# Projections by feature as three 256-column products in one PSUM bank, in place of a 512-column and a 256-column product whose halves VectorE adds

## The chip, the cores and the metric

The kernel runs on one core of a Trainium2 chip. The metric is the device time of one execution in microseconds; the times given are medians of several executions, and the profile is of one execution.

## The reference

The reference is one decoder layer with two parallel token mixers on 256 tokens of width 2048. All of it is in float32.

```python
h = rms_norm(x, pre_norm_w)                       # (256, 2048)
proj = h @ w_in                                   # one projection, 12304 columns
gdn_qkv, gdn_z, gdn_b, gdn_a, moba_qkv, moba_z, gate_a, gate_b = split(proj)
# A: causal depthwise conv (4 taps) and SiLU on q, k, v; l2-normed q, k;
#    gated delta rule in chunks of 64 tokens, 8 heads of 128; gated RMS norm
qkv = silu(causal_depthwise_conv(gdn_qkv, conv_w))
u_a = gated_rms(gated_delta_rule(...), gdn_z) @ w_branch_a
# B: causal softmax attention, 8 heads of 128 (one block of 256 tokens)
u_b = (attention(qb, kb, vb) * silu(moba_z)) @ w_branch_b
merged = sigmoid(gate_a) * u_a + sigmoid(gate_b) * u_b
out = x + rms_norm(merged @ w_out, post_norm_w)
```

## The kernel before

Every large product is made with operands that are split in two: a value is rounded to `hi` (float32r), and `lo` is the rest. A product is then hi·hi + hi·lo + lo·hi. `split` (L220) does this for weights: ScalarE copies to `hi` (L225), VectorE subtracts to get `lo` (L226). The normed and transposed input is held the same way in `hT`: for each of the 16 k-tiles of 128 input features, 512 columns, of which the first 256 (`S`, one for each token) are the high part and the last 256 the low part.

There are two kinds of projection. `proj_n` (L358) is by token: the input is the stationary operand, the weights stream, and three products of up to 512 columns for each k-tile and each half of the tokens add up in one bank. `proj_t` (L340) is by feature: the weights are stationary (128 features) and the tokens stream, because the convolution along the tokens and the scores need features on partitions. It handles 256 columns of `w_in`, that is two heads (`m`), in two loads of eight k-tiles (`kb`). For each k-tile `hi` is multiplied with all 512 columns of `hT`, so that hi·hi lies in the left half of the bank and hi·lo in the right, and `lo` with the first 256 columns, added to the left half:

```python
mm(pts[m], hi[:, kk, :], hT[:, k, :], start=(k == 0), stop=False)
mm(pts[m][:, :S], lo[:, kk, :], hT[:, k, :S], start=False, stop=(k == KT - 1))
```

Afterwards `halves` (L459) adds the two halves of the bank: ScalarE copies the right one to SBUF (L461), VectorE adds the left one (L462). `conv_silu` (L465) then multiplies by the tokens' norm factor `rrow` into a padded row `xp` (L468), and makes the four taps and the SiLU in place. `keys` (k), `queries` (q) and `values` (v) do that for the first mixer. `attention` (L1077) takes the queries `mq` as they come from `halves`, and the keys `mk` scaled by `rrow` (L1084). `attend` makes the scores `ms` from them later. The first four heads' keys come from `first_products` (L282), which is written out at the start of the kernel: four 512-wide products for the four heads of a k-tile, then four 256-wide ones; they use `halves` too.

The order of the blocks is the list `ORDER` (L42), beginning with q0, mv0, zg0, q1 and so on; `proj_t` is called 18 times (q, v, mq and mk four times each, k twice). All TensorE instructions keep program order (`mm`, `tr`, L146 to L150). Smaller work (scores, the inverse, attention, weighting) stands in queues of generators (`Queue`, L47) that are advanced by `tick` every few products, so it is interleaved with the projections by count of products, not by time. The other engines' instructions are put in order by a scheduler, unless they are pinned. PSUM has four banks of 512 columns for the projections (`acc`) and four for the rest (`aux`). Weights are loaded by the sync engine's queue, one megabyte at a time, into three buffers.

Of the kernel before, what the change touches and what calls it, by code (L numbers as in the profile page):

```python
# [8 lines left out]
F32 = mybir.dt.float32  # L9
# [3 lines left out]
ALU = mybir.AluOpType  # L13
AX = mybir.AxisListType

P = 128
# [58 lines left out]
def hybrid_layer(  # L75
# [15 lines left out]
    nc = tc.nc  # L91
    B, S, D = x.shape
    NT = S // P
    KT = D // P
    H = a_log.shape[1]
    HD = gdn_norm_w.shape[1]
    GW = H * HD
    NTAP = conv_w.shape[1]
# [21 lines left out]
    wf = early.enter_context(tc.tile_pool(name="wf", bufs=8))  # L120
# [3 lines left out]
    def acc_tile(name):  # L124
        return acc.tile([P, 512], F32, tag="acc", name=name)
# [4 lines left out]
    gq, vq, mq = Queue(), Queue(), Queue()  # L130
# [8 lines left out]
    def tick():  # L139
        after[0] -= 0.5  # L140
        for q in (gq, vq, mq, *(() if held else aq + bq), *extra):
            q.tick()
# [3 lines left out]
    def mm(*args, **kwargs):  # L146
        return pin(nc.tensor.matmul(*args, **kwargs))  # L147
# [72 lines left out]
    def split(raw, shape, name):  # L220
        splits[0] += 1
        pool = fourth[0] if fourth and splits[0] % 4 == 0 else wspl
        hi = pool.tile(shape, F32R, tag="hi", name=f"hi_{name}")
        lo = pool.tile(shape, F32R, tag="lo", name=f"lo_{name}")
        nc.scalar.copy(hi, raw)  # L225
        nc.vector.tensor_tensor(lo, raw, hi.bitcast(F32), op=ALU.subtract)  # L226
        return hi, lo
# [5 lines left out]
    hT = big.tile([P, KT, 2 * S], F32R, tag="hT", name="hT")  # L233
# [3 lines left out]
    def turn(c):  # L237

        pts = []
        for k in range(4 * c, 4 * c + 4):  # L240
            if k % 2 == 0:
                pt = aux_tile(f"hTp_{k}")
            pts.append((k, pt[:, k % 2 * S : (k % 2 + 1) * S]))
            for t in range(NT):
                tr(pts[-1][1][:, t * P : (t + 1) * P], xs[t][:, k * P : (k + 1) * P], ident)
        return pts
# [48 lines left out]
    pts = turn(0)  # L295
# [26 lines left out]
    rrow = cst.tile([P, S], F32, name="rrow")  # L322
# [16 lines left out]

    def proj_t(col, name):  # L340

        pts = [acc_tile(f"a_{name}_{m}") for m in range(2)]
        for kb in range(2):
            raw = wraw.tile([P, 8, 256], F32, tag="raw", name=f"raw_{name}_{kb}")
            nc.sync.dma_start(
                raw, w_in[kb * 1024 : (kb + 1) * 1024, col : col + 256].rearrange("(k p) c -> p k c", p=P)
            )
            for m in range(2):
                hi, lo = split(raw[:, :, m * P : (m + 1) * P], [P, 8, P], f"{name}_{kb}_{m}")
                for kk in range(8):  # L350
                    k = kb * 8 + kk
                    mm(pts[m], hi[:, kk, :], hT[:, k, :], start=(k == 0), stop=False)
                    mm(pts[m][:, :S], lo[:, kk, :], hT[:, k, :S], start=False, stop=(k == KT - 1))
                    if kk % 4 == 3:
                        tick()
        return pts
# [27 lines left out]
    late = []  # L384
# [71 lines left out]
        decaying.pop()  # L456


    def halves(pt, name):  # L459
        y = wf.tile([P, S], F32, tag="f256", name=f"y_{name}")  # L460
        nc.scalar.copy(y, pt[:, S:])  # L461
        nc.vector.tensor_tensor(y, pt[:, :S], y, op=ALU.add)  # L462
        return y

    def conv_silu(y, m, late=None):  # L465
        xp = xps[xpi[0] % 3]
        xpi[0] += 1
        nc.vector.tensor_tensor(xp[:, NTAP - 1 :], y, rrow, op=ALU.mult)  # L468
        nc.scalar.activation(y, xp[:, 0:S], AF.Copy, scale=pcol[:, m : m + 1])
        for j in range(1, NTAP):  # L470
            nc.vector.scalar_tensor_tensor(
                y, xp[:, j : j + S], pcol[:, j * NCV + m : j * NCV + m + 1], y, op0=ALU.mult, op1=ALU.add
            )
        if late is None:
            nc.scalar.activation(y, y, AF.Silu)
        else:
            late.append(lambda: pin(nc.scalar.activation(y, y, AF.Silu)))
# [26 lines left out]
    def score_pair(h, kT, qT):  # L504
        kqs = []
        for m in range(2):
            kq = big.tile([P, 2, 2 * S], F32R, tag=("tt", "tw")[m], name=f"kq_{h + m}")
            for i, y in enumerate((kT[m], qT[m])):
                nc.scalar.copy(kq[:, i, :S], y)
                nc.vector.tensor_tensor(kq[:, i, S:], y, kq[:, i, :S].bitcast(F32), op=ALU.subtract)  # L510
            kqs.append(kq)
        yield SC_WAIT
        for m in range(2):
            yield from scores(h + m, kqs[m], qT[m])

        for b in range(4):
            t, p_ = b // 2, b % 2
            c0 = t * 4 * P + p_ * 64
            nc.gpsimd.dma_start(
                l_d[b, h : h + 2].rearrange("h j i -> j h i"),  # L520
                gsl[h // HG][p_ * 64 : p_ * 64 + 64, h % HG : h % HG + 2, c0 : c0 + 64],
            )
# [78 lines left out]
    kTs = [[] for _ in range(H // 2)]  # L601

    def keys(p):
        pk = proj_t(CK + 2 * p * P, f"k{2 * p}")
        kTs[p] += [halves(pk[m], f"k{2 * p + m}") for m in range(2)]
        for m in range(2):
            conv_silu(kTs[p][m], H + 2 * p + m)

    def queries(p):
        h = 2 * p  # L610
        pq = proj_t(CQ + h * P, f"q{h}")
        qTs = [halves(pq[m], f"q{h + m}") for m in range(2)]
        for m in range(2):
            conv_silu(qTs[m], h + m)
        gq.add(score_pair(h, kTs[p], qTs))
        if p == H // 2 - 1:
            gq.add(inverse())
            gq.add(solve())
# [60 lines left out]
    def v_tok(h, vT):  # L679
        yield V_WAIT if h % 2 == 0 else 0.5  # L680
        while sc_left[0]:
            yield 1
        pv = aux_tile(f"vt_{h}")
        for t in range(NT):
            tr(pv[:, t * P : (t + 1) * P], vT[:, t * P : (t + 1) * P], ident)
        nc.vector.tensor_tensor(
            gvt[h // HG][:, :, h % HG, :],
            pv[:, : 2 * P].rearrange("p (t e) -> p t e", t=NT),
            sk[:, :, h : h + 1].to_broadcast([P, NT, P]),
            op=ALU.mult,  # L690
        )
# [3 lines left out]
    def values(p):  # L695
        h = 2 * p
        pv_ = proj_t(CV + h * P, f"v{h}")
        vTs = [halves(pv_[m], f"v{h + m}") for m in range(2)]
        for m in range(2):
            conv_silu(vTs[m], 2 * H + h + m)  # L700
            vq.add(v_tok(h + m, vTs[m]))
        v_left[0] -= 1
        after[0] = SLOW
# [373 lines left out]
    def attention(p):  # L1077
        h = 2 * p
        pq = proj_t(CMQ + h * P, f"mq{h}")
        qTs = [halves(pq[m], f"mq{h + m}") for m in range(2)]  # L1080
        pk = proj_t(CMK + h * P, f"mk{h}")
        kTs = [halves(pk[m], f"mk{h + m}") for m in range(2)]
        for m in range(2):
            nc.vector.tensor_tensor(kTs[m], kTs[m], rrow, op=ALU.mult)  # L1084
        for m in range(2):
            aq[m].add(attend(h + m, qTs[m], kTs[m]))

# [20 lines left out]
    late.append(lambda: silu_out("zg", ZG[2], GW, pzg))  # L1108
    gq.add(decays())
    for m in range(4):  # L1110
        conv_silu(kTs[m // 2][m % 2], H + m, late)
    for blk in ORDER:
        n, c = blk[:2].rstrip("0123456789"), int(blk[-1])
        if n in ("q", "kq"):
            if n == "kq":
                keys(c)
            queries(c)
        elif n in ("zg", "zm"):
            silu_gate(n, c)
        elif n == "v":  # L1120
            values(c)
        elif n == "mv":
            attention_values(c)
        elif n == "mk":
            attention(c)
        elif n == "ua":
            branch_pair(c)
        else:
            sigmoid_gate(n, {"ga": CGA, "gb": CGB}[n], c)
        if n == "ua":  # L1130
            next_differences(*((wa, 2), (wo, 0))[c])
# [130 lines left out]
    pts = [acc_tile(f"a_y{c}_{t}") for t in range(NT)]  # L1262
# [5 lines left out]
    for t in range(NT):  # L1268
        for k in range(KT):
            hi, lo = parts[k // 2][0][:, k % 2], parts[k // 2][1][:, k % 2]  # L1270
# [35 lines left out]
```

## Time and profile before

| | us |
|---|---|
| median of three runs | 778.01 (776.86 to 778.92) |
| the profiled execution | 777.05 |
| its span | 775.4 |
| TensorE busy | 763.5 |
| VectorE busy | 565.2 |
| ScalarE busy | 436.1 |

In the profile PE is TensorE's matmul, PEld its weight load, DVE is VectorE, ACT ScalarE, POOL GpSimd, SP the sync engine. A group's row names line, engine, operation, output and inputs, the stationary tile's and the streamed tile's shape, and the count; then the busy time in us, the mean duration of one in ns, and the idle time of the engine just before them. Durations of matmuls overlap, as they are pipelined. The chain of waits follows the work that ended last back from the end; a piece of it is given by start, duration, engine, tile and line, and the number of instructions. The timeline gives start, duration and the instruction, with equal neighbours merged.

### The profile page before, as it was taken

Reading aid. Unit: us, or ns where it says so; the run is one execution under the profiler, and the core shown is the slowest. Engines: PE = TensorE matmul, PEld = TensorE weight load, DVE = VectorE, ACT = ScalarE, POOL = GpSimd, SP = SyncE. Lnnn points to the kernel's source line nnn. Section 1 sums busy time; section 2 is a strip of 40 time slices with the busy share of each in tenths; the row PEclk is TensorE's granted clock in tenths of the full one; section 3 lists DMA queues with packets and bytes.
Section 4 is the critical chain, followed back from the end, with each engine's and each line's share of the span. In section 5 each row is a group of like instructions: output and inputs, shape, how many; then the busy total and the mean of one; then the engine's idle time right before and its main releaser. Section 6 shows DMA issues by size and latency. Waiting matters only on the chain.

```text
span 775.4 us, 10348 instructions
## 1 busy us (share of the span) xinstructions
PE 763.5 (98%) x3923; PEld 650.2 (84%) x3923; DVE 565.2 (73%) x914; ACT 436.1 (56%) x654; POOL 33.5 (4%) x61
## 2 busy tenths in 40 slices
PE   8999999999999999999999999999999999999995
PEld 7898988899888888888889888788888888888884
DVE  5777669885878898775547886686658776888853
ACT  5676666657655664454447475654455544556731
POOL 3000001112000000002001000000000000000000
PEclk9999999999999999999999999999999999999999
DMA  8576675457655556668336556657644956375912
GB/s 302 173 238 214 188 213 170 136 166 220 202 179 202 177 188 196 198 180 217 109 97 217 178 173 216 242 205 251 212 163 152 386 172 212 111 286 193 333 54 109
DMA packets 93656, 151.87 MB, mean 196 GB/s; under 512 B 3237, under 2 KB 46886, under 8 KB 93094
## 3 DMA queue, kind: packets, MB, share of 16 engines
q1 hardware_dynamic: 88902, 134.42, 53.4%
q0 software_dynamic: 4128, 15.74, 6.0%
q10 hardware_dynamic: 576, 1.05, 0.4%
q8 instruction: 31, 0.51, 0.3%
q14 instruction: 19, 0.16, 0.1%
HBM read 148.04 MB, written 3.15 MB: 195 GB/s over the span
## 4 chain that ended last, share of the span: by engine, by line
PE 95%; ACT 2%; DVE 2%; DMA 1%; SPq 0%; issue 0%; DVEq 0%
PE a_gb L147 11%; PE a_y L147 11%; PE a_ga L147 11%; PE a_zg L147 6%; PE a_mq L147 6%; PE a_v L147 6%; PE a_mk L147 6%; PE a_ub L147 6%; PE a_zm L147 6%; PE a_mv L147 5%; PE a_k L147 5%; PE a_ua L147 5%; PE a_q L147 4%; PE sv L147 2%; PE s L147 1%; DMA x<-in_x_dram 1%
## 5 line engine op out<-in xcount | busy, mean ns | idle before, releaser
L147 PE MATMUL a_ga<-hi_ga,hT 128*128 128x512 f32 x256 | 81.9, 393 | 0.0
L147 PE MATMUL a_gb<-hi_gb,hT 128*128 128x512 f32 x256 | 80.2, 390 | 0.0
L226 DVE TENSOR_TENSOR lo_gb<-raw_gb,hi_gb 128x1024 fp32r<-128x1024 f32 x32 | 38.9, 1223 | 25.1 <-ACT hi_gb L225 24.9
L147 PEld LDWEIGHTS a_gb<-hi_gb,hT 128*128 128x128 f32 x256 | 48.0, 188 | 10.6
L147 PEld LDWEIGHTS a_ga<-hi_ga,hT 128*128 128x128 f32 x256 | 48.1, 188 | 10.1
L225 ACT CAST hi_gb<-raw_gb 128x1024 fp32r<-128x1024 f32 x32 | 33.3, 1051 | 35.6 <-PE a_gb L147 26.5
L225 ACT CAST hi_ga<-raw_ga 128x1024 fp32r<-128x1024 f32 x32 | 33.7, 1055 | 34.0 <-PE a_ga L147 16.2
L226 DVE TENSOR_TENSOR lo_ga<-raw_ga,hi_ga 128x1024 fp32r<-128x1024 f32 x32 | 39.0, 1222 | 18.5 <-ACT hi_ga L225 18.3
L147 PE MATMUL a_ga<-lo_ga,hT 128*128 128x512 f32 x128 | 50.0, 391 | 0.1
L147 PE MATMUL a_gb<-lo_gb,hT 128*128 128x512 f32 x128 | 50.0, 391 | 0.0
L147 PE MATMUL a_zg<-hi_zg,hT 128*128 128x348 f32 (+1 forms) x192 | 47.0, 322 | 0.0
L147 PE MATMUL a_mq<-hT,hi_mq 128*128 128x512 f32 x128 | 46.8, 407 | 0.0
L147 PE MATMUL a_mk<-hT,hi_mk 128*128 128x512 f32 x128 | 46.1, 402 | 0.0
L147 PE MATMUL a_y<-hi_y,mT 128*128 128x512 f32 x144 | 46.1, 392 | 0.0
L147 PE MATMUL a_q<-hT,hi_q 128*128 128x512 f32 x128 | 46.0, 399 | 0.0
L147 PE MATMUL a_v<-hT,hi_v 128*128 128x512 f32 x128 | 45.3, 399 | 0.0
L147 PE MATMUL a_ub<-hi_ub,obT 128*128 128x512 f32 x128 | 41.3, 395 | 0.0
L147 PE MATMUL a_k<-hT,hi_k 128*128 128x512 f32 x128 | 40.6, 399 | 0.5 <-ACT hi_k L278 0.5
L147 PE MATMUL a_zm<-hi_zm,hT 128*128 128x512 f32 x128 | 40.5, 392 | 0.0
L147 PE MATMUL a_mv<-hi_mv,hT 128*128 128x512 f32 x128 | 40.1, 391 | 0.0
L147 PE MATMUL a_v<-hT,lo_v 128*128 128x256 f32 x128 | 35.9, 281 | 0.0
L147 PE MATMUL a_q<-hT,lo_q 128*128 128x256 f32 x128 | 35.9, 281 | 0.0
(377 smaller groups left out, 1972.8 us busy)
## 6 DMA issues: line engine op xcount, KB each, us to landing
raw_ga<-in_w_in_dram SPq DMA_DIRECT2D x16, 1024.0 KB, 5.1
raw_gb<-in_w_in_dram SPq DMA_DIRECT2D x16, 1024.0 KB, 5.7
raw_y<-in_w_out_dram SPq DMA_DIRECT2D x15, 1024.0 KB, 5.9
raw_q<-in_w_in_dram SPq DMA_DIRECT2D x8, 1024.0 KB, 5.6
raw_mv<-in_w_in_dram SPq DMA_DIRECT2D x8, 1024.0 KB, 5.1
raw_v<-in_w_in_dram SPq DMA_DIRECT2D x8, 1024.0 KB, 5.7
raw_zm<-in_w_in_dram SPq DMA_DIRECT2D x8, 1024.0 KB, 5.0
raw_mq<-in_w_in_dram SPq DMA_DIRECT2D x8, 1024.0 KB, 5.8
```

What stands on the lines that cost most here:

```text
L147: return pin(nc.tensor.matmul(*args, **kwargs))
L225: nc.scalar.copy(hi, raw)
L226: nc.vector.tensor_tensor(lo, raw, hi.bitcast(F32), op=ALU.subtract)
```

## The change

For each k-tile, `hi` is now multiplied with the two halves of `hT` in two products of 256 columns, and both, and that of `lo`, add up in the same 256 columns of the bank. The bank's result is complete, so `halves` is no longer called behind `proj_t`. `conv_silu` reads the bank directly in its multiplication by `rrow` (its new argument `src`), and so does the scaling of the `mk` keys. The `mq` queries, which need no scaling, are copied from the bank by ScalarE. The first products and their four `halves` stay as they are.

```diff
     def proj_t(col, name):
-        pts = [acc_tile(f"a_{name}_{m}") for m in range(2)]
+        pts = [acc_tile(f"a_{name}_{m}")[:, :S] for m in range(2)]
...
-                    mm(pts[m], hi[:, kk, :], hT[:, k, :], start=(k == 0), stop=False)
-                    mm(pts[m][:, :S], lo[:, kk, :], hT[:, k, :S], start=False, stop=(k == KT - 1))
+                    mm(pts[m], hi[:, kk, :], hT[:, k, :S], start=(k == 0), stop=False)
+                    mm(pts[m], hi[:, kk, :], hT[:, k, S:], start=False, stop=False)
+                    mm(pts[m], lo[:, kk, :], hT[:, k, :S], start=False, stop=(k == KT - 1))
...
+    def features(name):
+        return wf.tile([P, S], F32, tag="f256", name=f"y_{name}")
+
...
-    def conv_silu(y, m, late=None):
+    def conv_silu(src, y, m, late=None):
...
-        nc.vector.tensor_tensor(xp[:, NTAP - 1 :], y, rrow, op=ALU.mult)
+        nc.vector.tensor_tensor(xp[:, NTAP - 1 :], src, rrow, op=ALU.mult)
...
-        kTs[p] += [halves(pk[m], f"k{2 * p + m}") for m in range(2)]
+        kTs[p] += [features(f"k{2 * p + m}") for m in range(2)]
         for m in range(2):
-            conv_silu(kTs[p][m], H + 2 * p + m)
+            conv_silu(pk[m], kTs[p][m], H + 2 * p + m)
...
     def attention(p):
...
-        qTs = [halves(pq[m], f"mq{h + m}") for m in range(2)]
+        qTs = [features(f"mq{h + m}") for m in range(2)]
+        for m in range(2):
+            nc.scalar.copy(qTs[m], pq[m])
         pk = proj_t(CMK + h * P, f"mk{h}")
-        kTs = [halves(pk[m], f"mk{h + m}") for m in range(2)]
+        kTs = [features(f"mk{h + m}") for m in range(2)]
         for m in range(2):
-            nc.vector.tensor_tensor(kTs[m], kTs[m], rrow, op=ALU.mult)
+            nc.vector.tensor_tensor(kTs[m], pk[m], rrow, op=ALU.mult)
```

`queries` and `values` are changed as `keys` is.

More of the change, by code (lines that the diff above doesn't have):

```diff
@@ L611, in queries @@
         pq = proj_t(CQ + h * P, f"q{h}")
-        qTs = [halves(pq[m], f"q{h + m}") for m in range(2)]
+        qTs = [features(f"q{h + m}") for m in range(2)]
         for m in range(2):
-            conv_silu(qTs[m], h + m)
+            conv_silu(pq[m], qTs[m], h + m)
         gq.add(score_pair(h, kTs[p], qTs))
@@ L697, in values @@
         pv_ = proj_t(CV + h * P, f"v{h}")
-        vTs = [halves(pv_[m], f"v{h + m}") for m in range(2)]
+        vTs = [features(f"v{h + m}") for m in range(2)]
         for m in range(2):
-            conv_silu(vTs[m], 2 * H + h + m)
+            conv_silu(pv_[m], vTs[m], 2 * H + h + m)
             vq.add(v_tok(h + m, vTs[m]))
@@ L1110, in hybrid_layer @@
     for m in range(4):
-        conv_silu(kTs[m // 2][m % 2], H + m, late)
+        conv_silu(kTs[m // 2][m % 2], kTs[m // 2][m % 2], H + m, late)
     for blk in ORDER:
```

## The prediction

> **What bounds the kernel now.** I read the page's busy shares, its slices and the chain of waits first, then the list of what TensorE waited for.
>
> ```profile
> PE 763.5 (98%) x3923; PEld 650.2 (84%) x3923; DVE 565.2 (73%) x914; ACT 436.1 (56%) x654; POOL 33.5 (4%) x61
> PEclk9999999999999999999999999999999999999999
> PE 95%; ACT 2%; DVE 2%; DMA 1%; SPq 0%; issue 0%; DVEq 0%
> ...
> PE hTp L150 <- DMA x<-in_x_dram: 1.5, 2, 0.9
> PE warm L147 <- DVE epst L181: 1.1, 1, 1.1
> PE ms L147 <- DVE y_mk L1084: 0.7, 1, 0.7
> PE a_k L147 <- ACT hi_k L278: 0.5, 1, 0.5
> ```
>
> TensorE is busy 98% of the span at an almost full granted clock, and the chain that ends last is 95% TensorE. A busy row alone says little, since matmuls overlap; the list of waits says more. In 775.4 us TensorE waited 3.8 us, of which 3.1 us lie in the start, before the projections that the diff touches. In the rest of the kernel there is one wait, 0.7 us, for `y_mk`. So work taken off VectorE and ScalarE cannot buy more than that 0.7 us where the waits are shown; what counts is what TensorE itself must stream, and at which pace.
>
> The groups by line and shape give how many matmuls the change touches.
>
> ```profile
> L147 PE MATMUL a_mq<-hT,hi_mq 128*128 128x512 f32 x128 | 46.8, 407 | 0.0
> L147 PE MATMUL a_mk<-hT,hi_mk 128*128 128x512 f32 x128 | 46.1, 402 | 0.0
> L147 PE MATMUL a_q<-hT,hi_q 128*128 128x512 f32 x128 | 46.0, 399 | 0.0
> L147 PE MATMUL a_v<-hT,hi_v 128*128 128x512 f32 x128 | 45.3, 399 | 0.0
> L147 PE MATMUL a_k<-hT,hi_k 128*128 128x512 f32 x128 | 40.6, 399 | 0.5 <-ACT hi_k L278 0.5
> L147 PE MATMUL a_v<-hT,lo_v 128*128 128x256 f32 x128 | 35.9, 281 | 0.0
> ```
>
> The mean of one, 399 ns at 512 columns and 281 at 256, is a latency, not a price: by it a pair would take 680 ns. The price is the pace from start to start. The chain of waits gives it where one projection runs without interruption (start, us, what, how many).
>
> ```profile
> 138.26 11.31 PE a_k L147 x64
> ...
> 181.10 33.92 PE a_v L147 x192
> ```
>
> 64 matmuls are 32 pairs of one 512-wide and one 256-wide: 11.31 us / 32 = 353.4 ns a pair; 33.92 / 96 = 353.3. So a k-tile of `proj_t` costs 353 ns today, half of what the group means suggest.
>
> **Part 1: TensorE's products.** `proj_t` runs for q, v, mq and mk four times each (512 k-tiles by the rows above) and for k twice; the other 64 of a_k's 128 belong to the first products, which stay. That is 18 projections of 32 k-tiles, 576 in all. Each loses one 512-wide matmul and gains two 256-wide ones: the same 768 columns, one matmul and one weight load more. In the built program TensorE's order is otherwise unchanged. What must be found is the pace of 256-wide matmuls that follow one another. The trace has no long row of them, but rows of four in the first products, where each has weights of its own (timeline).
>
> ```profile
> 9.23 0.64 PE L147 MATMUL a_k<-hT,lo_k 128*128 128x256 f32 x4
> 9.70 1.09 PE L147 MATMUL a_k<-hT,hi_k 128*128 128x512 f32 x4
> ...
> 27.60 0.64 PE L147 MATMUL a_k<-hT,lo_k 128*128 128x256 f32 x4
> 28.07 1.09 PE L147 MATMUL a_k<-hT,hi_k 128*128 128x512 f32 x4
> ```
>
> Four take 0.47 us, 118 ns each. The other bound comes from wider matmuls that run without end in a projection by token, 512 columns in a_mv and 348 in a_zg.
>
> ```profile
> 63.50 20.45 PE a_mv L147 x90
> 83.95 15.35 PE a_zg L147 x96
> ...
> L147 PE MATMUL a_zg<-hi_zg,hT 128*128 128x348 f32 x128 | 31.6, 323 | 0.0
> ```
>
> 20.45 us / 90 = 227.2 ns and 15.35 / 96 = 159.9 ns. The line through them has 0.410 ns a column and some 17 ns that do not depend on the width; at 256 columns it gives 122 ns. The fixed 17 ns is what one matmul more should cost if the line holds. The lowest price is that of a 256-wide matmul behind a 512-wide one.
>
> ```profile
> 50.07 0.40 PE L147 MATMUL a_q<-hT,hi_q 128*128 128x512 f32 x1
> 50.30 0.28 PE L147 MATMUL a_q<-hT,lo_q 128*128 128x256 f32 x1
> ...
> 61.17 0.29 PE L147 MATMUL pg<-sp,tri_u 128*128 128x16 f32 x2
> ```
>
> 32 pairs from 50.07 to 61.17 are 346.9 ns each; 0.23 us of it is the 512-wide one, so 117 ns are left for the other. (This first projection is faster than the others by 6 ns a pair, for which I see no cause.) The k-tile after the change is then between 3 x 117 = 351 ns and 3 x 122 = 366 ns, against 353.3: from -2.3 to +12.7 ns, times 576 from -1.3 us to +7.3 us. I take 119.5 ns, a little above the 118 of the same width and operand, since the first of each four there follows a 512-wide one and the new rows never end: 358.5 ns, +5.2 ns, x 576 = +3.0 us. The first projection starts from 347 instead of 353, 32 x 6 ns = +0.2 us more. Sum: **+3.2 us**.
>
> Here the Trainium skill can be weighed against the rows. "TensorE: Matmul & The Clock Gate", section "Back-to-back issue gap", gives N / 2.4 + 2.5 ns for a warm matmul; an estimate by it is 215.8 ns for 512 columns and 109.2 for 256, so that the change would cost 2.5 ns a k-tile, 1.4 us in all. The trace does not agree with the level: 227.2 ns at 512.
>
> **Part 2: the weight loads.** 576 loads are added. Each is recorded at 188 ns.
>
> ```profile
> L147 PEld LDWEIGHTS a_q<-hT,lo_q x128: 187/189/192, 50.1 to 162.9; 128*128 128x128 f32 x128
> ```
>
> If a load could start only when the one before had ended, the rows of four could not run at 118 ns each; their loads overlap one another or the record holds a latency. I cost the loads at nothing beyond the pace above; the cover is the 118 to 122 ns of streaming. Were it gone, a k-tile would take 3 x 188 = 564 ns (rival 4).
>
> **Part 3: ScalarE and VectorE.** 36 half-sums go (18 projections of two banks). Tile and line views give the prices:
>
> ```profile
> L461 ACT COPY y_q<-a_q x8: 361/366/375, 60.3 to 164.0; 128x256 f32<-128x256 f32 x8
> L462 DVE TENSOR_TENSOR y_q<-a_q,y_q x8: 414/418/427, 61.5 to 164.9; 128x256 f32<-128x256 f32 x8
> L468 DVE TENSOR_TENSOR xp<-y_q,rrow x8: 415/416/421, 63.1 to 165.6; 128x256 f32<-128x256 f32 x8
> ```
>
> VectorE loses 36 x 0.418 = 15 us. ScalarE loses 36 copies and gains 8 (the `mq` features, which need no scaling), 28 x 0.366 = 10 us. The multiplication by `rrow` now reads the bank: L462, which reads a bank too, takes 418 ns and L468, which does not, 416, so that is free. None of it lies on the path, by the list of waits, except at one place.
>
> **Part 4: the one wait.** After the last `mk` projection the scores of its heads wait for the keys (VectorE's and TensorE's timelines):
>
> ```profile
> 439.07 0.41 DVE L462 TENSOR_TENSOR y_mk<-a_mk,y_mk 128x256 f32<-128x256 f32 x1
> 439.40 1.21 DVE L747 TENSOR_TENSOR tq_z<-tq_z,tq_g 128x1024 f32<-128x1024 f32 x1
> 440.53 0.42 DVE L1084 TENSOR_TENSOR y_mk<-y_mk,rrow 128x256 f32<-128x256 f32 x1
> ...
> 439.51 0.82 PE L147 MATMUL ms<-y_mk,y_mq 128*128 128x128 f32 x4
> 441.00 0.92 PE L147 MATMUL ms<-y_mk,y_mq 128*128 128x128 f32 x4 [0.68 <-DVE y_mk L1084]
> ```
>
> The half-sum and the scaling stand in VectorE's queue with a 1.21 us subtraction between them. After the change one operation makes the keys straight from the bank, and in the built order it stands ahead of the splits `lo_ga_1_0` and of those subtractions, so it runs as soon as the projection ends, well before the scores. The wait goes: **-0.7 us**. Next late there is nothing that the list shows.
>
> **Part 5: a wait that moves.** The first reader of a bank is now VectorE, in order: `xp<-a_.._0` stands ahead of the next block's second `lo` split, and `xp<-a_.._1` ahead of its third. Bank 0 is ready eight k-tiles (2.8 us) before its projection ends, and the split behind it is wanted 12 matmuls after the end at the earliest (1.9 us at a_zg's pace, the shortest); bank 1 is ready at the end, and the split behind it is wanted 24 matmuls later, 3.8 us. One read of 0.42 us and one split of 1.2 us fit. For the first projection `xp<-a_q_0` stands even ahead of the first split, `lo_mv_0_0`, with 2.8 us for both. I cost this at nothing; if the cover fails, a split comes late by about one read, 0.4 us, at up to 18 places.
>
> The sum is +3.2 - 0.7 = **+2.5 us**. The profiled execution took 777.05 us (its span of 775.4 and 1.65 around it) and would take 779.5; the median of the three runs is 0.96 us above it, 778.01, so the forecast for the median is 780.5, 0.3% more. A measurement of this kernel can tell about 0.3%, 2.3 us, from no change, and the forecast lies just over that.
>
> **Rivals.**
> 1. The forecast: 256-wide matmuls in an unbroken row take 119.5 ns or more and slow TensorE. For it: the line through 512 and 348. Against: the rows of four give 118. From 119.3 ns on, the result is over 0.3%. At 122 ns it is +7.3 + 0.2 - 0.7 = +6.8 us, 784.8. Chance 0.48.
> 2. No change: the pace stays at 118 ns. A k-tile takes 354 ns, +0.4 us in all, +0.2 for the first projection, and the wait's 0.7 us cancels it: 777.9. The skill's rule for the gap, named above, leads to the same case: 1.4 - 0.7 = +0.7 us, 778.7. Chance 0.41.
> 3. Faster: the price of a 256-wide matmul is 117 ns or less, and the freed 15 us of VectorE and 10 us of ScalarE also shorten delays too small for the list of waits. At 117 ns: -1.3 - 0.7 = -2.0 us, 776.0; with 1 us of small delays gone, 775.0. Against it: the unbroken pairs at 353.3 ns hold no visible waits. Chance 0.09.
> 4. The weight load becomes the bound. At 188 ns each, three a k-tile, 564 - 353 = 211 ns x 576 = +121 us, 899. The rows of four at 118 ns speak against it. "TensorE: Matmul & The Clock Gate", section "LDWEIGHTS (loading the stationary operand)", gives columns / 1.2 ns, by which 128 columns take 107 ns: an estimate just under the streaming, and so a warning that 256 columns are near the width at which loads show. Chance 0.01.
> 5. The splits come late (part 5): 18 x 0.4 us = 7.2 us on top of the forecast at worst, 788. Chance 0.01.
>
> **How the numbers follow.** Slower by over 0.3%: rivals 1, 4 and 5, 0.50. Within 0.3%: rival 2, 0.41. Faster: 0.09. The likeliest single case is the forecast, 780.5; alone it runs from 780.3 to 784.8. Since the second case has almost as much, the range takes it in and goes down to 776.8, in the faster one; it ends at 784.8, the line's price. About 1 in 10 is left out, half on each side.
>
> **What would show it.** In the profile of the changed kernel, the chain's unbroken a_v piece (96 k-tiles, 288 matmuls) should take 96 x 0.3585 = 34.4 us instead of 33.92; 34.0 would speak for rival 2 and under 33.7 for rival 3. The loads of a_q should still be recorded near 188 ns and the clock near full. TensorE's wait for `y_mk` should be gone, and no wait for `lo_` tiles (L226) should have come. The half-sum's groups should be down to the four of the first keys. The forecast is wrong if the pace of a row of 256-wide matmuls differs from that of rows of four, or if the 0.7 us comes back as a wait elsewhere.

## The result and the profile after

| | before | after | ratio, 95% interval |
|---|---|---|---|
| median of 6 runs each | 777.95 us | 780.65 us | 1.0037 (1.0025 to 1.0049) |
| the same two kernels again, beside the experiments (21 and 5 runs) | 777.48 us | 781.08 us | 1.0048 (1.0034 to 1.0062) |
| span of the profiled execution | 775.4 us | 778.3 us | |

The changed kernel is slower by 2.7 us in the first comparison and 3.6 us in the second. The forecast was 780.5 us.

The page of the changed kernel begins as follows (busy time, share of the span, instructions), with the list of what TensorE waited for below it.

```profile
PE 767.6 (99%) x4499; PEld 681.8 (88%) x4499; DVE 556.1 (71%) x878; ACT 426.9 (55%) x626; POOL 33.5 (4%) x61
...
PE warm L147 <- DVE epst L181: 1.1, 1, 1.1
PE hTp L150 <- DMA x<-in_x_dram: 0.8, 2, 0.4
PE a_k L147 <- ACT hi_k L278: 0.5, 1, 0.5
PE a_k L147 <- DVE lo_k L279: 0.4, 1, 0.4
```

There are 576 matmuls and 576 weight loads more, 36 instructions fewer on VectorE and 28 on ScalarE. The wait for `y_mk` is gone; all that TensorE still waited for lies in the start. The x and first-weight waits there are a little shorter than in the profile before (2.8 against 3.1 us with the warm-up's), in instructions that the change does not touch.

The chain of waits (start, us, what, count) has the same two unbroken pieces as before:

```profile
138.77 11.52 PE a_k L147 x96
...
182.05 34.56 PE a_v L147 x288
```

34.56 us / 288 = 120.0 ns a matmul, and 11.52 / 96 is 120.0 too. A k-tile takes 360.0 ns instead of 353.3. In the first projection (timeline) it is the same:

```profile
49.67 0.40 PE L147 MATMUL a_q<-hT,hi_q 128*128 128x256 f32 x2
49.90 0.28 PE L147 MATMUL a_q<-hT,lo_q 128*128 128x256 f32 x1
...
61.18 0.29 PE L147 MATMUL pg<-sp,tri_u 128*128 128x16 f32 x2
```

11.51 us from 49.67 to 61.18, against 11.10 before. By these unbroken pieces TensorE's part would be 576 x 6.7 ns = 3.8 us, and 0.2 us more because that projection started from a faster pace: 4.0 us. It is more, because other projections started from the faster pace too, late in the kernel for example. One piece of the chain there, before and after:

```profile
359.61 4.16 PE a_mk L147 x24
...
362.14 4.32 PE a_mk L147 x36
```

Both are 12 k-tiles: 346.7 ns each before and 360.0 after, 13.3 ns more. What all 576 k-tiles cost together is read below from the run that has the products alone.

At the place of the wait, VectorE's and TensorE's timelines now read:

```profile
439.08 0.42 DVE L1090 TENSOR_TENSOR y_mk<-a_mk,rrow 128x256 f32<-128x256 f32 x1 [0.69 <-PE a_mk L147]
440.04 1.23 DVE L226 TENSOR_TENSOR lo_ga<-raw_ga,hi_ga 128x1024 fp32r<-128x1024 f32 x1 [0.54 <-ACT hi_ga L225]
...
442.98 1.22 DVE L751 TENSOR_TENSOR tq_z<-tq_z,tq_g 128x1024 f32<-128x1024 f32 x1
...
443.43 1.47 PE L147 MATMUL ms<-y_mk,y_mq 128*128 128x128 f32 x8
```

The keys are made at 439.08, when their projection ends, and the eight matmuls of both heads' scores run as one row from 443.43, where before the second head's four started 1.49 us after the first's. The next product of `a_ga` tells what that is worth to TensorE, before and after:

```profile
441.57 0.59 PE L147 MATMUL a_ga<-hi_ga,hT 128*128 128x512 f32 x1
...
444.55 0.58 PE L147 MATMUL a_ga<-hi_ga,hT 128*128 128x512 f32 x1
```

From the first score to that product there are 2.06 us before (439.51 to 441.57) and 1.12 us after (443.43 to 444.55): 0.94 us less, where the list of waits had 0.7.

### The profile page after: what moved, and what is told of

It reads as the page before. It is cut to its first block, busy times and chain, and to the rows that moved or that the text cites. A ratio compares the mean times of both kernels' runs of the same rounds, so it can differ in the third digit from the quotient of the medians.

```text
span 778.3 us, 11438 instructions
## 1 busy us (share of the span) xinstructions
PE 767.6 (99%) x4499; PEld 681.8 (88%) x4499; DVE 556.1 (71%) x878; ACT 426.9 (55%) x626; POOL 33.5 (4%) x61
## 4 chain that ended last, share of the span: by engine, by line
PE 97%; DVE 1%; ACT 1%; DMA 0%; issue 0%; SPq 0%; DVEq 0%
PE a_gb L147 11%; PE a_ga L147 11%; PE a_y L147 11%; PE a_mq L147 6%; PE a_mk L147 6%; PE a_v L147 6%; PE a_q L147 6%; PE a_zg L147 6%; PE a_k L147 6%; PE a_ub L147 6%; PE a_mv L147 6%; PE a_zm L147 6%; PE a_ua L147 5%; PE sv L147 2%; PE s L147 1%; PE po L147 1%
## 5 line engine op out<-in xcount | busy, mean ns | idle before, releaser
L147 PE MATMUL a_mq<-hT,hi_mq 128*128 128x256 f32 x256 | 47.8, 288 | 0.0
L147 PE MATMUL a_mk<-hT,hi_mk 128*128 128x256 f32 x256 | 47.2, 286 | 0.0
L147 PE MATMUL a_q<-hT,hi_q 128*128 128x256 f32 x256 | 47.0, 285 | 0.0
L147 PE MATMUL a_v<-hT,hi_v 128*128 128x256 f32 x256 | 46.2, 283 | 0.0
L147 PE MATMUL a_k<-hT,hi_k 128*128 128x256 f32 (+1 forms) x192 | 41.0, 323 | 0.5 <-ACT hi_k L278 0.5
L147 PEld LDWEIGHTS a_mq<-hT,hi_mq 128*128 128x128 f32 x256 | 40.0, 192 | 0.5 <-issue 0.3
L147 PEld LDWEIGHTS a_v<-hT,hi_v 128*128 128x128 f32 x256 | 40.1, 192 | 0.1
```

## The experiments

**The two halves of the change, each by itself.** The first experiment takes the three products alone: the second goes to the right half of the bank, and the halves are added as before. The second takes the other engines' relief alone: the old two products, with only the left half of the bank read. Both are compared with the same runs of the kernel before, and the changed kernel was run again beside them.

```diff
 # products only (against the kernel before)
-  mm(pts[m], hi[:, kk, :], hT[:, k, :], start=(k == 0), stop=False)
-  mm(pts[m][:, :S], lo[:, kk, :], hT[:, k, :S], start=False, stop=(k == KT - 1))
+  mm(pts[m][:, :256], hi[:, kk, :], hT[:, k, :256], start=(k == 0), stop=False, ...)
+  mm(pts[m][:, 256:], hi[:, kk, :], hT[:, k, 256:], start=False, stop=(k == KT - 1), ...)
+  mm(pts[m][:, :S], lo[:, kk, :], hT[:, k, :S], start=False, stop=(k == KT - 1), ...)
 # relief only (against the changed kernel): the two old products, and
-  return pts
+  return [pt[:, :S] for pt in pts]
```

> The changed kernel once more, beside the experiments. Both theories: 2.7 us over the kernel before (ratio 1.0035), unbroken projections at 120.0 ns a matmul (11.52 us for 96).

> Kernel before with the 512-wide product cut into two of 256 columns, each into its own half of the bank; the halves are still added as before. Theory (TensorE pays for one matmul more in each k-tile, and the only gain is the 0.7 us wait for the last keys): projections as in the changed kernel, 120 ns a matmul, the wait stays; +3.7 to +4.4 us, about 782. Rival (part of the cost comes from the new order on VectorE and ScalarE, where the first reader of a bank is VectorE): +2 us or less.

> The changed kernel's other engines with the old products: 512 and 256 columns, and only the left half of the bank is read, so the product of the weights' high part with the input's low part is left out of the result. Theory: the half-sums buy only the wait for the last keys, -0.7 to -1.0 us, about 777.1. Rival (15 us less on VectorE and 10 us less on ScalarE also shorten delays that the list of waits does not show): -2 us or more.

| | median, us | ratio to before, 95% interval |
|---|---|---|
| before (21 runs) | 777.48 | |
| the changed kernel (5) | 781.08 | 1.0048 (1.0034 to 1.0062) |
| products only (5) | 781.74 | 1.0056 (1.0044 to 1.0069) |
| relief only (11) | 776.91 | 0.9993 (0.9984 to 1.0002) |

By the medians the products cost 4.3 us and the relief gains 0.6 us; together that is 3.7 us, and the changed kernel measured 3.6. The relief alone can't be told from no change by its interval, which reaches down to -1.2 us; the 2 us of its rival lie outside. The profile of products only has the pace of the changed kernel and the wait of the kernel before (chain of waits, then the list of waits):

```profile
139.05 11.52 PE a_k L147 x96
182.33 34.56 PE a_v L147 x288
...
PE ms L147 <- DVE y_mk L1085: 0.7, 1, 0.7
```

In that of relief only, TensorE's list of waits has nothing behind the start. So the slowdown is the products', and most of what VectorE and ScalarE give back lies at that wait; the profiles put numbers to both below.

**The wait alone.** In the kernel before, the scaling of the last pair of keys was held in program order, which puts both ahead of the 1.2 us subtraction.

```diff
-  nc.vector.tensor_tensor(kTs[m], kTs[m], rrow, op=ALU.mult)
+  (pin if p == 3 else id)(nc.vector.tensor_tensor(kTs[m], kTs[m], rrow, op=ALU.mult))
```

> Kernel before with the scaling of the last pair of mk keys held in program order, so that VectorE does it ahead of the 1.2 us subtraction. Theory: the scores of the last head start about 0.6 us earlier, -0.5 us, 777.4; the wait row for y_mk shrinks to 0.3 us or less. Rival (something else holds TensorE at that place): no change in the wait.

The wait fell from 0.7 to 0.2 us, as expected:

```profile
PE ms L147 <- DVE y_mk L1084: 0.2, 1, 0.2
```

The time did not follow to be seen: 777.94 us in 11 runs, ratio 1.0004 (0.9995 to 1.0013). The 0.5 us looked for is 0.06%, less than the medians can tell.

The profiles can tell it. Two stretches of the chain are compared: from the start of the first a_zg piece to the start of the last a_y piece, which leaves out the start of the kernel; and from the last product of `a_ga` ahead of the last heads' scores to the first one behind them. The ends of the first stretch, before and then with products only:

```profile
34.89 15.35 PE a_zg L147 x96
...
696.20 71.34 PE a_y L147 x312
...
34.74 15.33 PE a_zg L147 x96
...
700.45 71.35 PE a_y L147 x312
```

| profile of | first stretch, us | against before | at the scores, us |
|---|---|---|---|
| before | 661.31 | | 2.29 |
| the changed kernel | 664.60 | +3.29 | 1.35 |
| products only | 665.71 | +4.40 | 2.29 |
| relief only | 660.05 | -1.26 | 1.34 |
| keys in order | 660.55 | -0.76 | 1.81 |

With the keys in order TensorE is through with the scores 0.48 us sooner, the length by which the wait fell; without the wait it is 0.94 us sooner. The wait was thus worth at least its length on TensorE's path. The products cost 4.4 us in all 576 k-tiles, 7.6 ns each. The changed kernel is 1.1 us better than products only, of which 0.9 lie at the scores. (In relief only and keys in order the rest, some 0.3 us, is the faster pace of a few pairs, of which more below.)

**The pace against the width.** Why does a 256-wide matmul take 120 ns: because of a fixed part that each matmul pays, or because of a floor under the time of any matmul, which the expectations below put down to its weight load? The 512-wide product was cut at other places, at the same total of 768 columns a k-tile.

```diff
 # products only, cut at 384 (or 320) instead of 256
-  mm(pts[m][:, :256], hi[:, kk, :], hT[:, k, :256], ...)
-  mm(pts[m][:, 256:], hi[:, kk, :], hT[:, k, 256:], ...)
+  mm(pts[m][:, :384], hi[:, kk, :], hT[:, k, :384], ...)
+  mm(pts[m][:, 384:], hi[:, kk, :], hT[:, k, 384:], ...)
```

> Kernel before with the 512-wide product cut into 384 and 128 columns instead of 256 and 256; halves added as before. Theory A (a matmul costs its columns at 0.41 ns and a fixed 13 to 17 ns, whatever its width): 360 to 366 ns a k-tile, the same as with 256 and 256, about +4 us, 782. Theory B (a matmul cannot follow the one before in less than about 120 ns, because of its weight load, and 256 columns lie just at that floor): the 128-wide one costs 120 instead of 67, a k-tile about 173 + 120 + 120 = 413 ns, +34 us, 812.

> As the run before with 320 and 192 columns. Theory A: 360 to 366 ns a k-tile, about 782. Theory B: 147 + 120 + 120 = 387 ns, +19 us, 797.

They measured 811.55 us (ratio 1.0438, 1.0421 to 1.0455) and 798.50 us (1.0267, 1.0251 to 1.0282), so there is a floor: without one, by theory A, both would have taken about 782. Both totals lie near theory B's numbers. The chain of waits gives an unbroken projection in each, first 384 and 128, then 320 and 192:

```profile
320.96 13.02 PE a_v L147 x96
...
317.12 12.05 PE a_v L147 x96
```

That is 406.9 and 376.6 ns a k-tile. Theory B asked for 413 and 387: a floor of 120 ns is too high. With 120 for the 256-wide one and the line of the prediction for the widest (174.7 ns at 384, 148.4 at 320) there remain 112 and 108 ns for the narrow ones. That the totals fit theory B all the same is in part chance: by these paces the 576 k-tiles cost 31 and 13 us, and 34 and 21 were measured. In the second, TensorE's waits are 6.3 us in all, against 3.8 before; where the rest lies is open. A floor near 110 ns, with 256 columns just above it, would fit; that was tried directly, with all three products narrow in 14 of the 16 k-tiles.

```diff
 # against the changed kernel; 128 or 224 in place of W0
+  W = S if k in (0, KT - 1) else W0
-  mm(pts[m], hi[:, kk, :], hT[:, k, :S], start=(k == 0), stop=False)
-  mm(pts[m], hi[:, kk, :], hT[:, k, S:], start=False, stop=False)
-  mm(pts[m], lo[:, kk, :], hT[:, k, :S], start=False, stop=(k == KT - 1))
+  mm(pts[m][:, :W], hi[:, kk, :], hT[:, k, :W], start=(k == 0), stop=False, ...)
+  mm(pts[m][:, :W], hi[:, kk, :], hT[:, k, S : S + W], start=False, stop=False, ...)
+  mm(pts[m][:, :W], lo[:, kk, :], hT[:, k, :W], start=False, stop=(k == KT - 1), ...)
```

> The changed kernel with all three products 128 columns wide in the inner 14 of 16 k-tiles, so the second half of the tokens is left out there: narrow matmuls in an unbroken row. Theory F (a floor of about 110 ns a matmul, and 256 columns lie above it on the line of the wider ones): 109 to 112 ns a matmul, a k-tile 330 ns, about 15 us less than the changed kernel. Theory G (the floor is 120 ns and is what 256 columns pay): 120 ns, no change in time. Theory A (no floor): 69 ns by the line, until the splits of the weights become the bound.

> As the run before with 224 columns. Theories F and A: 107 to 112 ns a matmul, about 13 us less than the changed kernel. Theory G: 120 ns, no change in time.

The chains' unbroken projections, with 128 columns and with 224:

```profile
335.99 10.80 PE a_v L147 x96
...
319.11 10.81 PE a_v L147 x96
```

Twelve of the 96 matmuls are still 256 wide. Less these at 120 ns, 84 take 9.36 or 9.37 us: 111.4 and 111.5 ns, at 128 as at 224 columns. That is theory F: a floor at 111.5 ns, and 256 columns 8.5 ns above it. The line through the wider ones gives 122 at 256 and 109 at 224, so the two meet near 230 columns.

The expected times were missed. With one execution each, these kernels took 804.83 and 788.14 us where about 765 and 768 had been expected. TensorE then ran ahead of the splits in places and waited for them: its waits of all kinds are 8.0 us with 128 columns and 11.6 with 224, against 2.8 in the changed kernel. And the granted clock fell, as the last section shows: an estimate from windows of 10 us, each counted by what its clock lacks to 1.00, is 31 us lost with 128 columns and 7 with 224. Together that is most of the 39 and 20 us; the rest is open.

**The same weights twice in a row.** In the changed kernel the two `hi` products follow each other with the same stationary tile. Here `lo` was put between them.

```diff
   mm(pts[m], hi[:, kk, :], hT[:, k, :S], start=(k == 0), stop=False)
-  mm(pts[m], hi[:, kk, :], hT[:, k, S:], start=False, stop=False)
-  mm(pts[m], lo[:, kk, :], hT[:, k, :S], start=False, stop=(k == KT - 1))
+  mm(pts[m], lo[:, kk, :], hT[:, k, :S], start=False, stop=False)
+  mm(pts[m], hi[:, kk, :], hT[:, k, S:], start=False, stop=(k == KT - 1))
```

> The changed kernel with the lo product between the two hi products, so that no two neighbouring matmuls of a k-tile have the same weights. Theory (every matmul loads its weights, the same or not): no difference to the changed kernel, 780.6, 120 ns a matmul. Rival (the second load of the same weights is cheaper): 0.5 us or more slower.

780.96 us, ratio 1.0043 (1.0028 to 1.0058), as for the changed kernel; the unbroken piece is the same to the digit.

```profile
183.97 34.56 PE a_v L147 x288
```

So the order within a k-tile is free. (Its profile also has one wait of 0.6 us for a split, `lo_mv`, behind the small transfer of `grow`, for which VectorE waited 4.0 us there and 2.6 in the changed kernel; the chain of waits runs over that transfer.) At 256 columns the pace lies above the floor, where a cheaper load need not show; but the run with 128 columns also has two neighbours with the same weights in each k-tile, and its mean was 111.4 ns. A load of weights that are there already was not seen to cost less.

## Why the prediction was right

**What bounds the kernel.** TensorE's pace decided, as read from the list of waits. With relief only, 36 operations fewer on VectorE and 28 on ScalarE moved the median by 0.6 us and TensorE's path by 1.3 at most. The relief itself was smaller than forecast: by the two pages the changed kernel has 9.1 us less on VectorE and 9.2 on ScalarE, not 15 and 10. The prediction added up the records of single operations, and these overlap: in its own lines the subtraction at 439.40 begins before the half-sum of 439.07, 0.41 us long, has ended.

**Part 1, the products.** The forecast was 119.5 ns, 358.5 a k-tile, 34.4 us for the a_v piece and +3.2 us in all. Measured: 120.0, 360.0, 34.56 and +4.4. The mechanism was right: the same columns in one matmul more cost TensorE a little more for each k-tile. The line's fixed 17 ns would have been too much for it; measured were 7.6 ns. The pace lay between the two rows used as bounds, 118 from rows of four and 122 from the line. The sum is short by 1.2 us. Some 0.9 of it come from the pace, 0.5 ns a matmul, which was given to the row of the nearer width; the middle of the two bounds would have been right. The rows of four hold one matmul behind a 512-wide one, and that is the cheap one: in the profile before, the first of the four is followed after 115.5 ns in the mean, the second and third after 119.

The other 0.3 or so come from the pace before. The first projection's 347 ns a pair was taken as its own property, and 353.3 for all others. It is not its own: the a_mk piece at 359.61 us shown above has 346.7, and in the run with the keys in order, one more projection had it (chain of waits):

```profile
140.33 11.09 PE a_k L147 x64
```

64 matmuls in 11.09 us are 346.6 ns a pair, where the same a_k piece took 11.31 before. Pairs of 512 and 256 run at 347 or 353 ns; what chooses is open. The rows of 256 alone stayed at 120.0 in the four profiles that have them at that piece.

**Part 2, the weight loads.** They were costed at nothing beyond the pace, with the streaming as cover. That was right: loads of `a_q` are still recorded at 187 to 193 ns each, and matmuls follow one another every 120, so these records overlap and rival 4's 188 ns is no price. But there is a floor of 111.5 ns a matmul, not far under 120. What it consists of was not separated; that it is the weight load is likely and not shown. "TensorE: Matmul & The Clock Gate" in the Trainium skill, section "LDWEIGHTS (loading the stationary operand)", gives columns / 1.2 ns for a load, by which an estimate for 128 columns is 107 ns; the floor of 111.5 is 5 ns above it. The same page of the Trainium skill, section "Back-to-back issue gap", would give an estimate of 2.5 ns more a k-tile; measured were 6.7 in the unbroken pieces and 7.6 in the mean.

**Parts 3 and 4, the relief and the wait.** The wait went and nothing took its place. It was worth 0.94 us at the scores, more than the 0.7 us forecast: two rows of four, with the wait taken off, still took 0.26 us more than one row of eight. The medians (0.6 in relief only; 0.7 between products only and the changed kernel) are too coarse to tell 0.7 from 0.9.

**Part 5, the moved wait.** In the two profiles of the changed kernel no wait for a split came behind the projections.

**The sum.** 4.4 - 1.1 = 3.3 us by the measured terms, where the prediction had 3.2 - 0.7 = 2.5; the two comparisons gave 2.7 and 3.6. Both terms were too small and their errors cancel in part. That the forecast of 780.5 lies 0.15 us from the first median, 780.65, is luck: from its own base of 778.01 the measured terms lead to 781.3. And the prediction gave rival 2, no change, almost the same chance; the 2 ns between a pace of 118 and one of 120 decided between them.

## What to carry to other kernels

Cost a matmul by the pace from start to start in an unbroken piece of the chain, not by its mean duration: 281 ns was the record, 120 the price. A matmul more at the same number of columns has a price of its own, here 7.6 ns in the mean for each split of 512 into two of 256, and much more when a piece falls under the width at which the floor is met, here some 230 columns: cut at 384 the same columns cost 34 us. Taking 18 us of work off engines for which TensorE waits at one place only bought what that place was worth, about 1 us. An effect under 1 us that medians can't show can be read from the profiles, as a stretch between two instructions that stand in both; here two profiles of the same instructions can still differ by some 0.3 us, by the pace of the pairs.

## What the runs showed that was not expected

With 128 columns a matmul, TensorE's clock did not come back for a long time after a pause. In the values stage it waited 1.8 and 0.5 us for splits around 204 us. The windows of that run (PE busy, loads, VectorE, ScalarE, GpSimd, granted clock, DMA share, GB/s):

```profile
core 0: us, PE busy (x) PEld busy (x) DVE busy (x) ACT busy (x) POOL busy (x), PEclk, DMA share, GB/s
195.00:200.00 5.00, 5.00 (x47) 5.00 (x47) 2.36 (x2) 1.08 (x3) 1.96 (x4) 1.00 1.03 283
205.00:210.00 5.00, 4.56 (x22) 4.56 (x22) 3.91 (x9) 1.87 (x5) 0.00 (x0) 0.50 0.30 69
230.00:240.00 10.00, 10.00 (x49) 10.00 (x49) 2.92 (x4) 3.13 (x3) 0.00 (x0) 0.50 0.33 105
246.00:252.00 6.00, 6.00 (x25) 4.97 (x25) 4.22 (x10) 2.69 (x4) 0.00 (x0) 0.78 0.32 122
...
205.44 40.90 PE a_v L147 x190
```

For 40 us of busy TensorE the clock stayed at 0.50. The last line is the chain's piece there: 215 ns a matmul, 1.9 times the 111.4 at full clock. The clock rose only when the 512-wide products of a_ga followed at 246 us. With 224 columns the same kind of pause at this place was over within some 5 us:

```profile
205.00:210.00 5.00, 5.00 (x36) 5.00 (x36) 4.58 (x9) 1.86 (x4) 0.00 (x0) 0.75 0.71 207
210.00:215.00 5.00, 5.00 (x47) 5.00 (x46) 2.86 (x7) 2.66 (x5) 0.00 (x0) 1.00 0.63 201
```

An earlier pause, near 60 us, halved the clock in both runs (128 columns, then 224):

```profile
60.00:70.00 10.00, 9.18 (x36) 8.21 (x37) 8.39 (x16) 5.01 (x9) 0.00 (x0) 0.54 0.64 210
...
60.00:70.00 10.00, 8.83 (x34) 7.96 (x35) 7.96 (x14) 5.27 (x8) 0.00 (x0) 0.54 0.60 210
```

There some 5 us of narrow products, 224 columns as well as 128, did not lift it; it was back at about 71 us, some 4 us after the 512-wide products of a_mv had begun. So in the run with 128 columns a row of matmuls without gaps was not enough to lift the clock. Its matmuls stream less than half of the time at the floor's pace (128 columns of 0.41 ns in 111.5); whether that is the reason, and whether 224 columns are enough, is open. This is one execution of each kernel, and no run was made to settle it.
